# Attention in a transformer layer: two neighbouring score tiles of a first-half unit share one score buffer, one bank each

## The chip, the cores and the metric

The kernel runs on one core of a Trainium2 chip. The core's engines are named as in the profile: PE (TensorE, matmuls), DVE (VectorE), ACT (ScalarE), POOL (GpSimd) and SP (SyncE, which issues the DMAs here); PEld is PE's loading of weights. The metric is the device time of one execution in microseconds (us); the median over several runs is compared.

## The reference

One layer of an encoder for 1024 rows of 1024 values: adaptive normalisation, a mixer with two kinds of attention heads, a channel MLP. The change lies in the attention heads, which compute, cut to what matters:

```
# 8 latent heads (MLA), query/key width 96, value width 64; chunks of 64 rows, chunk-causal mask
s = q @ k.T * 96**-0.5;  s = where(key_chunk <= query_chunk, s, -1e30)
o = softmax(s) @ v
# 8 banded heads, width 64; each chunk sees itself and the 8 chunks before it, with a bias by distance
s = q @ k_band.T * 64**-0.5 + bias;  o = softmax(s) @ v_band
```

Everything is float32. Matmul operands are split into a high and a low part, and a product is made of three matmuls (high by high, high by low, low by high).

## The kernel before, in words

The sequence is cut into eight tiles of 128 query rows. A *unit* is one head and one half of the sequence: the first half (`u.g == 0`) has the tiles i = 0 to 3, the second half the tiles 4 to 7. There are 16 first-half and 16 second-half units. The banded units come first (`c00`, `c01`, ... in names: head pair, then odd or even head), then the latent units (`m00` to `m13`: group of four heads, then head). Halves and heads follow each other in the list `tiles`, and a loop calls `u.scores(i)` for tile n and, three tiles later, `u.values(i)` for a pair of tiles. Each call is followed by `pace`, which puts matmuls of other projections (the fillers: `ipq`, `ipv`, `mp`, `qu`, `ku`, `oc`) into the stream by the cost of what was just issued.

`Unit.scores` makes one tile: matmuls of queries by keys into a score buffer in PSUM (`s`), for query tile i over (i − lo + 1) × 128 keys; on DVE the mask and a minimum over the row (lines 810 to 822; the scores are kept negated); on ACT the exponential with a row sum (line 829); a reciprocal on DVE; a scaled float16 high part on POOL (line 73) and its low part on DVE (line 851); and a DMA that transposes both (line 863) into a tile `PT` that a pair of query tiles shares. `Unit.values` multiplies a pair's transposed tiles by the values on PE (line 891). After the last pair, ACT and DVE take the result out (lines 900 and 901) and a DMA stores it.

A score buffer is 1024 columns of float32, two PSUM banks of 512. There are two such buffers (tag `S`, `bufs=2`), which take four of the eight banks. A tile of a first-half unit has at most 512 columns and so fills at most the first bank of its buffer.

The order of instructions on each engine isn't the order of the code. A scheduler lays all instructions out with a timing model of its own, taking those of higher priority first: the calls of `tc.high_priority` lift scores by `OFF_S = 400` and the rest by 200. Each engine then works its list off strictly in order, and semaphores hold an instruction until what it needs is done. A buffer of a pool is handed to the next tile of its tag when the last reader of the tile before is done. Between two uses of one tile the framework adds the waits that it finds necessary.

The attention lies between 86 and 612 us of the span: banded heads up to about 340 us, latent heads from about 375 us.

## Time and profile before

| | |
|---|---|
| median of 3 runs | 1333.68 us (1331.05 to 1333.88) |
| profiled execution | 1334.5 us, span 1332.7 us |
| mean granted TensorE clock | 0.958 |
| instructions | 18710 |

The page's first part gives each engine's busy time and share of the span. In the rows by stage each engine has its busy time and count, and behind them the granted clock of PE (1.00 is full speed), the mean busy share of the DMA engines and the bandwidth. In a row of waits stand the waiting instruction, what released it, the total in us, how often, and the longest. In the timeline a row gives the start, how long it took, the engine and line, the output and inputs, a count of merged instructions, and in brackets the idle time before it and what ended it. A matmul's duration contains its way through the array; successive matmuls overlap.

### The profile page before, as it was taken

Reading aid. Unit: us, or ns where it says so; the run is one execution under the profiler, and the core shown is the slowest. Engines: PE = TensorE matmul, PEld = TensorE weight load, DVE = VectorE, ACT = ScalarE, POOL = GpSimd, SP = SyncE. Lnnn points to the kernel's source line nnn. Section 1 sums busy time; section 2 is a strip of 40 time slices with the busy share of each in tenths; the row PEclk is TensorE's granted clock in tenths of the full one; section 3 lists DMA queues with packets and bytes.
Section 4 is the critical chain, followed back from the end, with each engine's and each line's share of the span. In section 5 each row is a group of like instructions: output and inputs, shape, how many; then the busy total and the mean of one; then the engine's idle time right before and its main releaser. Section 6 shows DMA issues by size and latency. Waiting matters only on the chain.

```text
span 1332.7 us, 18710 instructions
## 1 busy us (share of the span) xinstructions
PE 1212.8 (91%) x6168; PEld 997.1 (75%) x6168; DVE 1088.7 (82%) x1928; ACT 622.3 (47%) x1132; POOL 572.3 (43%) x610
## 2 busy tenths in 40 slices
PE   3899999989667798888889999999999998999998
PEld 3888878868555576666677888888888886888886
DVE  6979898877589967894779888898889986687667
ACT  5454654445555545553366444444443444443331
POOL 5476773675675633354615445444444541000000
PEclk9899999989878798997999999999999998999999
DMA  8416768766123685879702333333333336943441
GB/s 321 144 55 156 164 143 197 150 151 138 35 72 70 119 172 122 152 164 326 275 16 79 106 124 111 122 116 108 113 106 132 111 119 221 393 151 114 132 159 63
DMA packets 223689, 190.57 MB, mean 143 GB/s; under 512 B 148708, under 2 KB 166884, under 8 KB 223592
## 3 DMA queue, kind: packets, MB, share of 16 engines
q1 hardware_dynamic: 223592, 189.38, 50.3%
q8 instruction: 48, 0.79, 0.3%
q14 instruction: 49, 0.40, 0.1%
HBM read 117.24 MB, written 37.49 MB: 116 GB/s over the span
## 4 chain that ended last, share of the span: by engine, by line
PE 48%; DVE 3%; DMA 2%; issue 1%; ACT 1%; POOL 0%; SPq 0%; POOLq 0%; DVEq 0%
PE p L1125 10%; PE p L1126 10%; PE p L1127 10%; PE dnA_P L1460 2%; PE dnA_P L1461 2%; PE dnA_P L1462 2%; PE dnB_P L1461 1%; PE dnB_P L1460 1%; PE dnB_P L1462 1%; PE dnA L1461 1%; PE dnA L1460 1%; PE dnA L1462 1%; PE dnB L1461 1%; PE dnB L1462 1%; PE dnB L1460 1%
## 5 line engine op out<-in xcount | busy, mean ns | idle before, releaser
L77 ACT ACTIVATE dnP<-dnr 128x1024 fp32r<-128x1024 f32 x73 | 77.4, 1064 | 117.5 <-PE dnA_P L1462 46.4
L1434 DVE TENSOR_TENSOR dnP<-dnr,dnP 128x1024 fp32r<-128x1024 f32 x72 | 87.9, 1224 | 52.7 <-ACT dnP L77 47.7
L73 POOL TENSOR_SCALAR hlm<-Pm,rim 128x512 f16<-128x512 f32 (+2 forms) x96 | 65.4, 691 | 77.5 <-DVE rim L832 32.0
L84 POOL TENSOR_TENSOR wf<-wu,wf 128x512 fp32r<-128x512 f32 x22 | 39.8, 1808 | 118.2 <-ACT wf L77 118.2
L1296 DVE SCALAR_TENSOR_TENSOR u<-c,cvp,u 128x1023 f32<-128x1023 f32 x44 | 58.6, 1372 | 27.8 <-ACT u L1295 27.8
L84 POOL TENSOR_TENSOR wb<-wu,wb 128x512 fp32r<-128x512 f32 x22 | 42.2, 1920 | 75.0 <-ACT wb L77 59.6
L73 POOL TENSOR_SCALAR hlc<-Pc,ric 128x640 f16<-128x640 f32 (+2 forms) x64 | 48.0, 753 | 54.5 <-DVE ric L832 25.8
L851 DVE SCALAR_TENSOR_TENSOR hlm<-Pm,rim,hlm 128x512 f16<-128x512 f32 (+2 forms) x96 | 65.9, 696 | 5.5 <-POOL hlm L73 5.2
L829 ACT ACTIVATE Pc<-sc,mc 128x640 f32<-128x640 f32 (+2 forms) x64 | 42.2, 660 | 55.2 <-DVE mc L818 26.1
L891 PE MATMUL pvm<-PTm,vt 128*128 128x256 f16 (+1 forms) x320 | 47.7, 302 | 22.1 <-DMA PTm<-hlm 14.2
L829 ACT ACTIVATE Pm<-sm,mm 128x128 f32<-128x128 f32 (+3 forms) x64 | 47.1, 738 | 37.7 <-DVE mm L822 21.2
L1295 ACT ACTIVATE u<-c,cvp 128x1024 f32<-128x1024 f32 x44 | 52.4, 1238 | 26.0 <-DVE c L1394 18.0
L1297 DVE SCALAR_TENSOR_TENSOR u<-c,cvp,u 128x1022 f32<-128x1022 f32 x44 | 61.7, 1442 | 0.0
L891 PEld LDWEIGHTS <-vt 128*128 128x128 f16 x320 | 33.1, 111 | 37.0 <-issue 21.6
L77 ACT ACTIVATE wc<-ws 128x512 fp32r<-128x512 f32 x21 | 13.3, 632 | 91.9 <-DVE ws L1144 86.1
L154 PE MATMUL ipq<-wq_s,hT 128*128 128x256 f32 x192 | 55.7, 290 | 0.0
L156 PE MATMUL ipq<-wq_s,hT 128*128 128x256 f32 x192 | 55.4, 288 | 0.0
L155 PE MATMUL ipq<-wq_s,hT 128*128 128x256 f32 x192 | 55.1, 287 | 0.0
L851 DVE SCALAR_TENSOR_TENSOR hlc<-Pc,ric,hlc 128x640 f16<-128x640 f32 (+2 forms) x64 | 49.2, 774 | 6.8 <-POOL hlc L73 6.7
L1461 PE MATMUL dnA_P<-dnP 128*128 128x512 f32 x132 | 51.3, 389 | 0.0
L1462 PE MATMUL dnA_P<-dnP 128*128 128x512 f32 x132 | 51.3, 389 | 0.0
L1460 PE MATMUL dnA_P<-dnP 128*128 128x512 f32 x132 | 51.2, 389 | 0.0
(442 smaller groups left out, 4413.7 us busy)
## 6 DMA issues: line engine op xcount, KB each, us to landing
wu<-w_up SPq DMA_DIRECT2D x44, 512.0 KB, 3.5
dnr<-g_d SPq DMA_DIRECT2D x73, 256.0 KB, 2.8
aw<-w_ada SPq DMA_DIRECT2D x48, 256.0 KB, 3.4
g_d<-u SPq DMA_DIRECT2D x22, 512.0 KB, 3.0
dnr<-w_down SPq DMA_DIRECT2D x44, 256.0 KB, 5.4
adaw<-w_ada_a SPq DMA_DIRECT2D x16, 512.0 KB, 6.0
x<-x SPq DMA_DIRECT2D x16, 512.0 KB, 9.8
g_d<-gs SPq DMA_DIRECT2D x22, 256.0 KB, 2.8
```

The costliest lines, as they stand in the source:

```text
L73: pool.tensor_scalar(o, i, s, 1.0, op0=MUL, op1=MUL)
L77: act.activation(o, i, AF.Copy)
L84: (pool if eng == "p" else dve).tensor_tensor(o, i, f32(hi), op=SUB)
L829: act.activation(pr[:, :n], sv, AF.Exp, bias=m[:], scale=-1.0, accum_out=rsum[:, 0:1])
L851: dve.scalar_tensor_tensor(hl[:, w:2 * w], pp, ri[:], hl[:, :w], op0=MUL, op1=SUB)
L1125: pe.matmul(pt, sh, pg[:, 0], start=(k == 0 and not add), stop=False, skip_group_check=skip)
L1126: pe.matmul(pt, sh, pg[:, 1], start=False, stop=False, skip_group_check=skip)
L1127: last = pe.matmul(pt, sl, pg[:, 0], start=False, stop=(k == 3), skip_group_check=skip)
L1434: r = f(*a, **k)
L1460: pe.matmul(pt, sh, w[:, 0, 0], start=start, stop=False, skip_group_check=add)
L1461: pe.matmul(pt, sh, w[:, 1, 0], start=False, stop=False, skip_group_check=add)
L1462: pe.matmul(pt, sl, w[:, 0, 0], start=False, stop=stop, skip_group_check=add)
```

## The change

In a first-half unit (i below 4) a buffer is taken only for the even tiles. The odd tile that follows writes the second half of the same buffer, which is its other bank. Second-half units keep one buffer for each tile. Nothing else is edited, and no matmul or transfer is added or left out.

```
-                s = ps.tile([P, 1024], F32, name=f"s{nm}", tag="S", bufs=2)
+                if i >= 4 or i % 2 == 0:
+                    u.s = ps.tile([P, 1024], F32, name=f"s{nm}", tag="S", bufs=2)
+                s = u.s if i >= 4 else u.s[:, i % 2 * 512:(i % 2 + 1) * 512]
```

The later lines move down by two (797 becomes 799, 803 becomes 805, 891 becomes 893). The scheduler lays everything from the first score tile to the end of the attention out anew. In the rows below, a name is followed by the unit and the query tile: `sc00_2` is the score buffer that was taken for tile 2 of unit `c00`. The size at the end tells the tile: 128 columns for tile 0, 256 for tile 1, 384 for tile 2, 512 for tile 3. What an instruction waits for stands in brackets where there is something: a counter of an engine (`Activation_49` is ACT's) or of a DMA queue.

The first unit of the banded heads on PE, before:

```order
L797 MATMUL sc00_0_904<-k0_0_897,qh0_0_0_888 128x128 [waits Activation_49,Pool_49]
L797 MATMUL sc00_0_904<-k0_0_897,ql0_0_890 128x128
L797 MATMUL sc00_1_926<-k0_0_897,qh0_0_0_888 128x256
L797 MATMUL sc00_1_926<-k0_0_897,ql0_0_890 128x256
L154 MATMUL ipv0_4_1026<-wv0_s0_518,hT0_0_1_259 128x256
...
L155 MATMUL ipv0_4_1026<-wv0_s0_518,hT0_0_1_259 128x256
L797 MATMUL sc00_2_949<-k0_0_897,qh0_0_0_888 128x384 [waits Activation_49]
L797 MATMUL sc00_2_949<-k0_0_897,ql0_0_890 128x384
```

And now:

```order
L799 MATMUL sc00_0_904<-k0_0_897,qh0_0_0_888 128x128 [waits Activation_49,Pool_49]
L799 MATMUL sc00_0_904<-k0_0_897,ql0_0_890 128x128
L799 MATMUL sc00_2_948<-k0_0_897,qh0_0_0_888 128x384
L799 MATMUL sc00_2_948<-k0_0_897,ql0_0_890 128x384
L154 MATMUL ipv0_4_1024<-wv0_s0_518,hT0_0_1_259 128x256
...
L154 MATMUL ipv0_4_1024<-wv0_s0_518,hT0_0_1_259 128x256
L799 MATMUL sc00_0_904<-k0_0_897,qh0_0_0_888 128x256 [waits Activation_49]
L799 MATMUL sc00_0_904<-k0_0_897,ql0_0_890 128x256
```

Tiles 1 and 2 have changed places: tile 2 follows tile 0 at once, and tile 1, which now lies in tile 0's buffer, waits on ACT's counter. The count that it waits for is that of tile 0's exponential.

The start of unit `m12` (a latent head, near 554 us) on PE, before:

```order
L803 MATMUL sm12_0_7029<-mk12_0_6946,mq12_0l_6938 128x128
L803 MATMUL sm12_1_7060<-mk12_0_6946,mq12_0h_6937 128x256 [waits Activation_49]
...
L803 MATMUL sm12_1_7060<-mk12_0_6946,mq12_0l_6938 128x256
L154 MATMUL oc6_0_7187<-wo4_0_5355,ch6_7183 128x512
...
L803 MATMUL sm12_2_7094<-mk12_0_6946,mq12_0h_6937 128x384 [waits Activation_49]
...
L803 MATMUL sm12_2_7094<-mk12_0_6946,mq12_0l_6938 128x384
L891 MATMUL pvm11_1_7045<-PTm11_4_0_6896,vt1_0_4955 128x256 [waits PE_49]
...
L891 MATMUL pvm11_1_7045<-PTm11_4_1_6901,vt1_4_5213 128x256 [waits DMAHW1_49]
```

And now:

```order
L805 MATMUL sm12_0_7001<-mk12_0_6918,mq12_0l_6910 128x128
L729 MATMUL mq13_0_ps_7193<-ident_68,qn1_0_4937 96x128 [waits DVE_49,PE_49]
...
L893 MATMUL pvm11_1_7017<-PTm11_4_0_6868,vt1_0_4939 128x256 [waits Activation_49]
...
L893 MATMUL pvm11_1_7017<-PTm11_4_1_6873,vt1_4_5195 128x256 [waits DMAHW0_49]
...
L805 MATMUL sm12_2_7065<-mk12_0_6918,mq12_0h_6909 128x384 [waits PE_49,Activation_49]
...
L805 MATMUL sm12_0_7001<-mk12_0_6918,mq12_0h_6909 128x256 [waits Activation_49]
...
L805 MATMUL sm12_0_7001<-mk12_0_6918,mq12_0l_6910 128x256
L154 MATMUL oc6_0_7157<-wo4_0_5337,ch6_7153 128x512
```

The 12 value matmuls of unit `m11` (`pvm11_1`), which stood behind tiles 1 and 2 and six `oc` matmuls, now stand ahead of them, four transposes (`mq13_0_ps`) after tile 0. On DVE, ACT, POOL and SP the score tiles keep the order 0, 1, 2, 3, 4.

## The prediction

> **What bounds the kernel now.** I read the page's busy times and chain first, then the busy times by stage, then the waits of the stage that has slack, then that stage's timeline.

> ```profile
> span 1332.7 us, 18710 instructions
> PE 1212.8 (91%) x6168; PEld 997.1 (75%) x6168; DVE 1088.7 (82%) x1928; ACT 622.3 (47%) x1132; POOL 572.3 (43%) x610
> PE 48%; DVE 3%; DMA 2%; issue 1%; ACT 1%; POOL 0%; SPq 0%; POOLq 0%; DVEq 0%
> ```

> TensorE (PE) is busy 91% of the span and carries nearly all that the chain of waits attributes, so only what makes PE idle, or run at a lower clock, moves the end. The profiled execution took 1334.5 us, 1.8 more than its span and 0.8 more than the median of 1333.7. Busy times by stage (PE, weight loads, DVE, ACT, POOL, then granted clock, DMA share, GB/s):

> ```profile
> 86.00:150.00 64.00, 62.12 (x461) 55.16 (x460) 55.13 (x178) 32.80 (x78) 38.66 (x47) 1.00 0.61 146
> 150.00:210.00 60.00, 55.91 (x398) 47.85 (x397) 55.33 (x147) 35.55 (x85) 42.07 (x49) 0.97 0.75 156
> 210.00:275.00 65.00, 62.82 (x461) 55.03 (x459) 55.41 (x147) 28.80 (x71) 34.27 (x41) 1.00 0.76 175
> 275.00:340.00 65.00, 59.02 (x325) 49.37 (x326) 46.35 (x127) 31.97 (x105) 42.59 (x92) 0.95 0.61 134
> 375.00:455.00 80.00, 55.74 (x253) 41.98 (x253) 72.32 (x214) 44.49 (x106) 49.80 (x53) 0.80 0.39 84
> 455.00:505.00 50.00, 47.80 (x258) 38.39 (x256) 37.32 (x97) 23.42 (x49) 23.96 (x30) 0.95 0.77 164
> 505.00:612.00 107.00, 85.88 (x485) 67.57 (x486) 85.11 (x214) 52.39 (x110) 42.75 (x60) 0.90 0.76 154
> 612.00:1333.00 721.00, 700.40 (x3044) 570.10 (x3043) 588.10 (x593) 311.56 (x415) 231.78 (x160) 0.99 0.42 144
> ```

> The first four rows are the banded heads: PE is full, because other projections' matmuls stand between the score tiles. In 375–455 (first latent heads) DVE is busy 72.32 of 80 us, so DVE sets the pace. In 505–612 (last four latent heads) no engine is full: PE idles 21.1 us and DVE 21.9. That stage is a ring of waits between engines, and the order on PE decides there. From 612 on nothing of the change is left. The waits of PE in 375–612, of PE in 86–340, and of DVE in 505–612 (total us, times, longest):

> ```profile
> PE sm L803 <- ACT Pm L829: 16.3, 15, 2.3
> PE pvm L891 <- DMA PTm<-hlm: 14.2, 9, 3.3
> ...
> PE pvc L891 <- DMA PTc<-hlc: 4.5, 5, 1.9
> PE sc L797 <- ACT Pc L829: 3.1, 3, 1.8
> ...
> DVE sm L821 <- PE sm L803: 10.7, 8, 2.5
> ```

> PE waits for two things: a score buffer that the exponential (L829) has to clear, 16.3 us, and a transposed tile that a DMA has to land before the value matmuls (L891), 14.2 us. The last row closes the ring: DVE in turn waits for score matmuls.

> **The change, part by part.** No operation is added or removed; two orders change.

> *Waits.* Before, each tile waits for the exponential of the tile two before it. Now tiles 0 and 1 share one buffer. In the built program tile 1's first matmul waits for tile 0's exponential although it writes the other bank; tile 3 waits for tile 2's in the same way; tile 2 is free as soon as the other buffer is. So still two tiles are in flight, and PE takes them as 0, 2, 1, 4, 3 where DVE, ACT, POOL and SP keep 0, 1, 2, 3, 4 (SP's transposes among them, so no queue is passed). A tile whose scores are ready on PE one place early gains nothing, since the other engines take it in the old place; tiles 1 and 3 come one place late.

> *Term a, the last four heads.* The start of head m12, in the trace of before on PE, with the two transposes on SP that matter for it:

> ```profile
> 553.79 0.42 PE L803 MATMUL sm<-mk,mq_0h 96*128 96x128 f32 x2
> 554.05 0.27 PE L803 MATMUL sm<-mk,mq_0l 96*128 96x128 f32 x1
> 556.35 0.50 PE L803 MATMUL sm<-mk,mq_0h 96*128 96x256 f32 x2 [2.04 <-ACT Pm L829]
> 556.69 0.28 PE L803 MATMUL sm<-mk,mq_0l 96*128 96x256 f32 x1
> 556.82 0.40 PE L154 MATMUL oc<-wo,ch 128*128 128x512 f32 x1
> ...
> 558.99 0.62 PE L803 MATMUL sm<-mk,mq_0h 96*128 96x384 f32 x2 [0.61 <-ACT Pm L829]
> 559.45 0.33 PE L803 MATMUL sm<-mk,mq_0l 96*128 96x384 f32 x1
> 559.63 1.38 PE L891 MATMUL pvm<-PTm,vt 128*128 128x256 f16 x12
> 560.84 0.60 PE L729 MATMUL mk_ps<-ident,kn 128*96 128x128 f32 x4
> 561.24 0.72 PE L803 MATMUL sm<-mk,mq_0h 96*128 96x512 f32 x2
> ...
> 555.75 1.24 SPq L863 DMA_TRANSPOSE PTm<-hlm  x1
> 557.09 2.58 SPq L863 DMA_TRANSPOSE PTm<-hlm  x2
> ...
> DMA to landing us min/median/max: 2.3/3.0/5.2
> ```

> Before, tile 1 (256 columns), six `oc` matmuls and tile 2 (384 columns) stand ahead of the 12 value matmuls of m11 at 559.63. They cover its transposes: the first was issued at 555.75 and lands at 558.1 to 558.8 by the last row; the second, issued at 557.09, lands at 559.4 to 560.1. In the changed order only four transposes (0.60) stand between tile 0 and these value matmuls. PE comes to them at 554.3 + 0.6 = 554.9 and stands until 558.8; it runs eight, waits for the second piece, and is through at about 560.4. Queued behind it on PE are tile 2 (0.8), four transposes (0.6), tile 1 (0.8) and six `oc` (six steps from 556.82 to about 558.2, 1.4), so that block ends at 564.0. Before, the same work without four transposes (0.6), which came later, ended at 561.2. The loss is 564.0 − 561.2 − 0.6 = 2.2 us, with the two waits of 2.04 and 0.61 already credited. For those tiles DVE waits next (the 10.7 row).

> Value groups move ahead of score tiles in this way at three places of the stage: m11's tiles 1 and 2, m12's tiles 1 and 2, and m12's tiles 3 and 4. 3 × 2.2 = 6.6 us. The lower end is 0, if the ring settles into another rhythm in which the transposes are there; the upper is the whole stand of 3.9 at each, 11.7. I take 6.6, whose rows are this place's own.

> *Term b, 375–455.* DVE sets the pace and keeps its order of tiles: 0, between −2 and +2 (a PE wait of 2.3, the longest in its row, either way).

> *Term c, the score-buffer waits of 16.3 us.* Tiles 2 and 4 shed theirs, tiles 1 and 3 take them up one exponential later: 0 beside what term a credits.

> *Term d, the banded heads.* Tiles 1 and 3 move behind 20 to 30 filler matmuls, and their transposes land later against the same value matmuls. All waits of this kind there are 4.5 + 3.1 = 7.6 us. I take +2, about a quarter more; from −3 (the 3.1 gone) to +6 (nearly doubled). The cover is the fillers; the place where they are thinnest is 275–340 (PE 59.02 of 65).

> *Term e, the clock.* In 505–612 the granted clock is 0.90 beside 21.1 us of PE idle: 10.7 us of clock lost, 0.5 per idle us. For 6.6 more idle I take half of that rate, +1.6; ends 0 and 3.3.

> [...]

> Sum: 1334.5 + 6.6 + 0 + 0 + 2 + 1.6 = 1344.7; against the median, 0.8 lower, **1344 us**. By the ends of a to e it reaches from 1329 to 1357.

> **Rivals.**

> *A, the clock tips over: about 1358.* If the stands of 3.9 come in full (11.7 instead of 6.6) and drop 505–612 to the clock of 375–455, its PE work grows by 85.88 × (0.90/0.80 − 1) = 10.7: 1334.5 + 11.7 + 2 + 10.7 = 1358.9, 1358 against the median. For: 375–455 shows that clock with waits of this kind. Against: 455–505 has its clock at 0.95 next to it. It decides where the stage's clock falls below 0.85.

> *B, faster: about 1326.* The buffer waits vanish and the transposes hold. Between tile 0 and tile 1 of m12 there now stand value matmuls, tile 2 and eight transposes, 1.38 + 0.8 + 1.2 = 3.4 us, where tile 2's wait for the same exponential ended 4.7 us after tile 0; it is mostly covered. If half of the 16.3 goes (8.2) and a, d and e stay at 0, 1334.5 − 8.2 = 1326.3, against the median 1325.5. Against it: PE reaches the value matmuls earlier, and 14.2 us of waits there say that they are not ready. It decides where that row stays at 14 or less.

> [...]

> *C, nothing: 1334.* The change doesn't loosen what it seems to (two tiles in flight before and after), and only the order of equals is swapped: terms a, d, e cancel against the shed waits.

> **How the numbers follow.** A measurement of this kernel tells 0.2% (2.7 us) from no change. Forecast 0.56, A 0.14, B 0.22, C 0.08. Faster is B, same is C, slower the forecast and A: 0.22, 0.08, 0.70. The range from 1327 to 1358 holds the forecast's own 1329 to 1357, C, half of B (which spreads from 1322 to 1331: 0.11 left out) and half of A (1354 to 1362: 0.07 left out), so 0.18 is outside.

> **What would show it.** Right: in the profile after, PE's waits for transposes in the latent heads rise from 14.2 towards 21, the waits for the exponential stay near 16, DVE's wait for scores passes 10.7, stage 505–612 becomes 7 to 9 us longer, the banded heads about 2, 375–455 and all from 612 on stay. Term a is wrong if the value waits stay; d if the banded stages move by over 6 us; e if the last stage's clock stays at 0.90. The forecast falls if 375–455 moves by over 4 us, since I hold DVE to set its pace, or if the whole is below 1331.

## Result: 0.4% slower, and the profile after

The changed kernel takes 1338.82 us (median of 20 runs, 1333.99 to 1346.63) where the kernel before takes 1333.67 in the same comparison. The ratio is 1.0039, 95% interval 1.0025 to 1.0053: slower by 5.2 us. A second comparison gave 1.0032 (1.0014 to 1.0050). The forecast was 1344, with 0.70 on slower; direction and range held, the size was 5 us too large. Line numbers of the changed kernel are two higher from the score buffer on.

The profiled execution of the changed kernel took 1335.7 us, 3.1 under the median, so its stages show where time went, not all of it. First its whole and the page's busy times, then busy times by stage in the windows of the prediction (PE, weight loads, DVE, ACT, POOL, granted clock, DMA share, GB/s):

```profile
span 1333.9 us, 18712 instructions
PE 1213.6 (91%) x6168; PEld 996.4 (75%) x6168; DVE 1094.3 (82%) x1928; ACT 622.5 (47%) x1132; POOL 582.0 (44%) x610
```

```profile
375.00:455.00 80.00, 57.99 (x268) 43.93 (x267) 75.33 (x224) 45.96 (x108) 52.69 (x54) 0.78 0.41 88
455.00:505.00 50.00, 47.92 (x258) 38.59 (x255) 42.15 (x96) 24.23 (x50) 24.85 (x30) 0.94 0.73 160
505.00:612.00 107.00, 82.57 (x457) 64.59 (x457) 82.92 (x206) 49.53 (x104) 42.83 (x58) 0.90 0.67 138
612.00:1333.00 721.00, 701.71 (x3060) 570.52 (x3060) 586.63 (x595) 313.28 (x418) 233.17 (x160) 0.99 0.43 146
```

Windows fixed in time mislead once work has moved: at 612 the changed kernel is still in its last head. So here are the stages cut at events (first banded scores, first latent transposes, first output projection `op`, first feed-forward product, first `dn`), first of before, then of after:

```profile
86.20:357.90 271.70, 251.63 (x1688) 216.78 (x1687) 221.43 (x626) 139.65 (x360) 166.37 (x241) 0.96 0.64 145
357.90:611.70 253.80, 200.41 (x1044) 155.22 (x1041) 209.68 (x572) 130.33 (x288) 124.95 (x149) 0.88 0.60 125
611.70:664.20 52.50, 48.80 (x210) 38.98 (x208) 35.01 (x29) 18.17 (x32) 30.97 (x28) 0.95 0.87 332
664.20:1114.50 450.30, 439.71 (x1914) 356.61 (x1913) 397.08 (x410) 212.64 (x307) 196.28 (x129) 0.99 0.31 105
```

```profile
84.90:358.70 273.80, 253.79 (x1689) 218.02 (x1687) 224.73 (x626) 138.97 (x360) 170.37 (x241) 0.95 0.63 143
358.70:619.00 260.30, 202.31 (x1042) 156.35 (x1040) 216.56 (x573) 132.05 (x289) 129.05 (x149) 0.87 0.57 122
619.00:670.70 51.70, 49.00 (x208) 38.62 (x208) 35.65 (x29) 17.05 (x31) 29.82 (x28) 0.95 0.88 334
670.70:1116.40 445.70, 437.85 (x1915) 355.36 (x1913) 392.00 (x410) 212.72 (x307) 198.60 (x129) 1.00 0.32 105
```

The latent heads (second row) grow by 6.5 us: 4.6 more idle (260.30 − 202.31 against 253.80 − 200.41), the rest a lower clock. The feed-forward stage (fourth row), which the change does not touch, shrinks by 4.6. That is the shape of the result: most of the forecast loss came, and nearly as much was given back where I had said that nothing of the change is left.

The waits of PE in 375–615, of PE in 86–340 and of DVE in 505–612:

```profile
PE pvm L893 <- DMA PTm<-hlm: 22.6, 13, 4.4
PE sm L805 <- ACT Pm L831: 13.9, 13, 2.5
```

```profile
PE pvc L893 <- DMA PTc<-hlc: 9.6, 6, 3.4
```

```profile
DVE sm L823 <- PE sm L805: 5.1, 7, 1.3
```

The first row answers to 14.2 before: waits for transposed tiles rose to 22.6, as forecast. The second answers to 16.3. The DVE row answers to 10.7 and fell, against the forecast.

### The profile page after: what moved, and what is told of

Same layout as the page of the kernel before. It is cut to its first block, busy times and chain, and to the rows that moved or that the text cites. A ratio compares the mean times of both kernels' runs of the same rounds, so it can differ in the third digit from the quotient of the medians.

```text
span 1333.9 us, 18712 instructions
## 1 busy us (share of the span) xinstructions
PE 1213.6 (91%) x6168; PEld 996.4 (75%) x6168; DVE 1094.3 (82%) x1928; ACT 622.5 (47%) x1132; POOL 582.0 (44%) x610
## 5 line engine op out<-in xcount | busy, mean ns | idle before, releaser
L73 POOL TENSOR_SCALAR hlm<-Pm,rim 128x512 f16<-128x512 f32 (+2 forms) x96 | 69.1, 731 | 87.9 <-DVE rim L834 28.6
L1298 DVE SCALAR_TENSOR_TENSOR u<-c,cvp,u 128x1023 f32<-128x1023 f32 x44 | 55.8, 1309 | 27.6 <-ACT u L1297 24.8
L853 DVE SCALAR_TENSOR_TENSOR hlm<-Pm,rim,hlm 128x512 f16<-128x512 f32 (+2 forms) x96 | 69.9, 742 | 7.2 <-POOL hlm L73 6.9
L893 PE MATMUL pvm<-PTm,vt 128*128 128x256 f16 (+1 forms) x320 | 45.8, 294 | 22.6 <-DMA PTm<-hlm 22.6
L1297 ACT ACTIVATE u<-c,cvp 128x1024 f32<-128x1024 f32 x44 | 52.3, 1238 | 23.4 <-DVE c L1396 16.5
L853 DVE SCALAR_TENSOR_TENSOR hlc<-Pc,ric,hlc 128x640 f16<-128x640 f32 (+2 forms) x64 | 54.3, 856 | 9.4 <-POOL hlc L73 9.1
L154 PE MATMUL ipq<-wq_s,hT 128*128 128x256 f32 x192 | 56.7, 295 | 0.0
L1299 DVE SCALAR_TENSOR_TENSOR u<-c,cvp,u 128x1022 f32<-128x1022 f32 x44 | 55.5, 1301 | 0.0
## 6 DMA issues: line engine op xcount, KB each, us to landing
dnr<-g_d SPq DMA_DIRECT2D x73, 256.0 KB, 2.8
aw<-w_ada SPq DMA_DIRECT2D x48, 256.0 KB, 3.5
dnr<-w_down SPq DMA_DIRECT2D x44, 256.0 KB, 5.4
g_d<-gs SPq DMA_DIRECT2D x22, 256.0 KB, 2.8
```

Source lines behind the costliest of these rows:

```text
L73: pool.tensor_scalar(o, i, s, 1.0, op0=MUL, op1=MUL)
L154: pe.matmul(pt, sh, mh, start=(start and i == 0), stop=False)
L853: dve.scalar_tensor_tensor(hl[:, w:2 * w], pp, ri[:], hl[:, :w], op0=MUL, op1=SUB)
L893: last = pe.matmul(dst, u.vst(j), mov, start=(x == 0), stop=(x == len(todo) - 1), skip_group_check=True)
L1298: dve.scalar_tensor_tensor(u[:, 1:], c[:, :S - 1], cvp[:, cv + 1:cv + 2], u[:, 1:], op0=MUL, op1=ADD)
```

## Experiments

Stage lengths come from the profiled execution of each run, cut at the same events; idle is length minus PE busy; lost clock is half of the half-clock stretches in the stage; transpose waits are PE's waits for transposed tiles in the latent heads to their end.

| run | median us, ratio (95%) | banded | latent: length, idle, lost clock | transpose waits | feed-forward |
|---|---|---|---|---|---|
| before | 1333.7 | 271.7 | 253.7, 53.4, 29.6 | 14.2 | 450.3 |
| before_again | 1331.9, one run | 271.9 | 252.0, 52.5, 31.6 | 14.5 | 448.8 |
| after | 1338.8, 1.0039 (1.0025–1.0053) | 273.8 | 260.4, 58.0, 34.8 | 22.6 | 445.6 |
| after_again | 1337.3, 1.0032 (1.0014–1.0050) | 276.8 | 259.9, 55.8, 36.3 | 20.6 | 444.5 |
| e1_latent_only | 1332.5, 0.9997 (0.9983–1.0011) | 274.1 | 256.5, 56.0, 32.7 | 17.9 | 444.5 |
| e2_banded_only | 1326.7, 0.9950 (0.9933–0.9967) | 277.0 | 250.6, 48.0, 35.1 | 12.4 | 446.0 |
| e3_in_order | 1344.3, 1.0081 (1.0059–1.0104) | 274.2 | 265.7, 63.1, 40.9 | 20.3 | 446.5 |
| e4_before_values_first | 1347.5, 1.0108 (1.0088–1.0127) | 273.0 | 271.5, 60.5, 47.0 | 23.4 | 444.4 |
| e5_after_values_later | 1336.0, 1.0014 (0.9995–1.0033) | 277.2 | 255.8, 51.9, 35.8 | 16.7 | 446.4 |
| e6_before_adds_first | 1330.8, 0.9985 (0.9968–1.0002) | 275.0 | 251.2, 53.0, 28.2 | 10.9 | 447.7 |
| e7_after_scalings_first | 1338.4, 1.0034 (1.0012–1.0056) | 275.2 | 255.5, 54.8, 32.7 | 17.4 | 446.5 |
| e8_values_later_adds_first | 1334.8, 1.0003 (0.9985–1.0022) | 277.3 | 256.0, 56.2, 32.0 | 14.6 | 447.3 |
| e9_before_split_first | 1331.4, 0.9986 (0.9970–1.0002) | 277.4 | 251.5, 51.8, 31.4 | 13.0 | 446.9 |
| e10_one_place | 1337.4, 1.0039 (1.0020–1.0059) | 274.9 | 260.6, 56.7, 38.6 | 22.2 | 446.8 |

Across the runs the latent heads' length goes with the transpose waits, from 250.6 us at 12.4 to 260.6 at 22.2; e3 and e4 lie above that line, with 41 and 47 us of clock lost. before_again, e6 and e9 have the PE order of before all through the attention, and after_again and e7 that of after. So the table also shows what one order varies by: transpose waits of 10.9 to 14.5 and latent heads of 251.2 to 253.7 us with the order of before, 17.4 to 22.6 and 255.5 to 260.4 with that of after.

The theory: PE comes to value matmuls before their transposed tiles have landed, because the shared buffer lets the scheduler put value groups ahead of score tiles. Rivals: the wait of tile 1 for tile 0's exponential by itself; PE's order of tiles, 0, 2, 1, against that of the other engines; the clock alone.

**Which heads (e1, e2).** The sharing in the latent heads alone, and in the banded heads alone:

```
-if i >= 4 or i % 2 == 0:
+if u.band or i >= 4 or i % 2 == 0:          # e1; s = u.s there too
+if not u.band or i >= 4 or i % 2 == 0:      # e2; s = u.s there too
```

> Shared score buffers in the latent heads alone; the banded heads are as before. Theory (the loss comes from value matmuls that PE reaches before their transposed tiles, in the last four latent heads): 1338 to 1341 us, +4 to +7; PE's waits for transposes in the latent heads above 20 us. Rival 1 (the banded heads lose it): within 0.2% of 1334. Rival 2 (the whole difference is the granted clock, which falls differently for any new order): anything from -5 to +5, with the waits no guide to it.

> Shared score buffers in the banded heads alone; the latent heads' score tiles keep a buffer each. Theory: within 0.2% of 1334 (term d said +2), PE's waits for transposes in the latent heads near 14 us. Rival 1 (the banded heads lose it): +4 to +6, 1338 to 1340. Rival 2 (granted clock): anything from -5 to +5.

Both missed, in the same direction. The latent sharing alone gave no loss, the banded sharing alone was 0.5% *faster* than before, the fastest kernel here, and together they lose 0.4%: the parts do not add up. Both also have the shorter feed-forward stage (444.5 and 446.0). With that set aside, e1's latent heads are still 3 to 5 us longer than the two of before, and e2's are shorter. Rival 2 (the clock) allowed anything from −5 to +5, so e1's time doesn't rule it out; its idle time in the latent heads, 56.0 where the order of before has 51.8 to 53.4, speaks against the clock as the whole. e2's latent gain lies in the first four latent heads, whose tiles it doesn't share: 127.8 us, where the order of before has 134.6 to 135.2 and e1 136.4. So the banded heads' sharing also changes what comes behind them. (e2's profiled execution, 1330.2 us, is the slowest of its six.)

**Value groups put ahead by hand, and put back (e4, e5).** e4 is the kernel before, with a buffer for each tile; in the latent heads tile 1 is issued behind the value group traced last, tile 3 behind the first eight matmuls of the next. e5 is the changed kernel, with the value groups of the second halves traced one tile later and issued behind the newest score tile.

```
+with tc.issue_after(vlast[-1]) if i in (1, 3) and not u.band and vlast else ...:   # e4, score matmuls
     ...
+late.append((u, i))       # e5, latent, u.g == 1; run at the next tile:
+with tc.issue_after(slast[-1]):
+    v.values(j)
```

> The kernel before, a buffer for each tile, with one thing of the change's PE order put in by hand: in the latent heads score tile 1 is issued behind the first group of value matmuls of the head before, and tile 3 behind the first part of the second. Theory (the order of value matmuls on PE is the loss, the shared buffer only brings it about): +3 to +7, 1337 to 1341, waits for transposes above 20 us. Rival (the loss is the wait of tile 1 for tile 0's exponential, which this kernel does not have): within 0.2% of 1334.

> The changed kernel with the second-half value groups of the latent heads issued one score tile later on PE, behind tiles 1 and 3 of the next head as in the kernel before. Shared buffers and their waits stay. Theory: the loss goes, 1331 to 1336, waits for transposes in the latent heads at 15 us or less. Rival (the wait of tile 1 for tile 0's exponential is the loss): 1337 to 1341, unchanged.

e4 loses 14 us with no shared buffer at all, twice what was expected; its latent heads are 18 us longer. Its waits for transposes, 23.4 us, are little more than the changed kernel's 22.6, so they are not the price by themselves. Its waits for score buffers fell at the same time, from 16.3 to 2.5, and idle time rose by 7. What e4 shows besides is a lower clock (same columns as above):

```profile
375.00:455.00 80.00, 59.91 (x252) 44.68 (x250) 73.83 (x216) 45.44 (x105) 55.46 (x55) 0.74 0.37 84
455.00:505.00 50.00, 46.32 (x239) 37.40 (x240) 36.19 (x92) 21.15 (x46) 18.15 (x25) 0.87 0.69 150
```

0.80 and 0.95 before have become 0.74 and 0.87: 47.0 us of clock lost in the latent heads where before lost about 30. In e5 the shared buffers and their waits stay (14.1 us for the exponential), and the waits for transposes are 16.7 (15 or less was expected). Its time lies some 3 us below the changed kernel's, with an interval that just holds 1 but overlaps both of the changed kernel's. Its profile helps little: idle time, 51.9, is below the 54.8 to 58.0 that the changed order shows, but e7, with the changed kernel's own order through the attention, shows 17.4 of transpose waits and 255.5 us of latent heads beside e5's 16.7 and 255.8. The order of value groups is thus enough to bring a loss (e4); that putting them back takes part of this one away is likely, but not shown.

**The wait or the order of tiles (e3).** Shared buffers, but every tile behind a shared pair issued in the old order:

```
+with tc.issue_after(odd_s[-1]) if (i < 4 and i % 2 == 0 or i == 4) and odd_s else ...:   # score matmuls
```

> The changed kernel, with the score tiles kept in their old order on PE (0, 1, 2, 3, 4) by issue order alone; the shared buffer and the wait of tile 1 for tile 0's exponential stay, and value groups still stand between tile 0 and tile 1. Theory (value matmuls ahead of their transposes): most of the loss stays, 1335 to 1342 us, waits for transposes in the latent heads at 17 us or more. Rival (the loss is PE taking tiles as 0, 2, 1, 4, 3 while the other engines keep 0 to 4): 1327 to 1332.

It is slower still, by 10.3 us. The rival that blames the order 0, 2, 1 by itself falls, since the old order with shared buffers is no faster. The theory's range was missed too (1342 at most). The shared wait doesn't show as the price: e3's waits for the exponential are 10.7 us, fewer than the changed kernel's 13.9. What grew is idle time (63.1) and lost clock (40.9), and as the edit lays out everything anew from the first banded unit on, why e3 is slower than the changed kernel stays open.

**The stage behind the attention (e6, e9, e7).** The scheduler's new layout reaches 60 us past the attention. On DVE before, the scalings of row tiles 5 and 6 come ahead of the residual add of tile 7 and of the split (`b<-hv,b`) that PE waits for; after, the add and the split come first. DVE in the first microseconds of the stage, which begins at 664.2 before and 670.7 after:

```profile
665.03 3.46 DVE L1193 TENSOR_SCALAR x<-x,r 128x1024 f32<-128x1024 f32 x2
668.42 2.28 DVE L1186 TENSOR_TENSOR x<-x,pa 128x1024 f32<-128x1024 f32 x1
670.62 1.28 DVE L84 TENSOR_TENSOR b<-hv,b 128x512 fp32r<-128x512 f32 x2
...
680.25 0.69 DVE L1222 TENSOR_TENSOR hv<-hv,hv 128x512 f32<-128x512 f32 x1 [5.45 <-ACT hv L1089]
```

```profile
671.35 2.29 DVE L1188 TENSOR_TENSOR x<-x,pa 128x1024 f32<-128x1024 f32 x1
673.56 1.78 DVE L84 TENSOR_TENSOR b<-hv,b 128x512 fp32r<-128x512 f32 x1
675.26 1.40 DVE L1195 TENSOR_SCALAR x<-x,r 128x1024 f32<-128x1024 f32 x2
...
681.82 0.69 DVE L1224 TENSOR_TENSOR hv<-hv,hv 128x512 f32<-128x512 f32 x1 [1.15 <-ACT hv L1091]
```

From the stage's start, the split begins at 6.4 before and 2.9 after, and `hv` comes at 16.0 before (14.5 in before_again) and 11.1 after. PE's waits for the split in this stage, before and after:

```profile
PE c_g L1126 <- DVE b L84: 4.2, 2, 2.5
```

```profile
PE c_g L1128 <- DVE b L84: 1.9, 2, 1.6
```

They fell by 2.3 us, and PE's idle time in the stage by 2.7, from 10.6 to 7.9. e6 puts the two scalings behind the add in the kernel before; e9 behind the split as well; both leave all that lies ahead as it was. e7 puts the scalings back ahead of the adds in the changed kernel.

```
+if t in (5, 6): continue                       # e6: scaled with tile 7,
+with tc.issue_after(add.ins): ...              #     behind its add
+with tc.issue_after(lo_ins["b11", 1].ins): ... # e9: tiles 5, 6 behind the split
+with tc.issue_after(scaled[...].ins): ...      # e7: adds of 4, 6, 7 behind scalings
```

> The kernel before with one thing put in by hand that the change brought along behind the attention: at the start of the feed-forward layer DVE issues the scalings of row tiles 5 and 6 behind the residual add of tile 7. Theory (the change also gives 4 to 6 us back there, which the prediction did not see): 1327 to 1330 us, the feed-forward stage 445 to 446 us where it was 450.3, its idle time near 8 us where it was 10.6. Rival (that stage's difference is where the granted clock happened to fall in the profiled runs): within 0.2% of 1333.

> The kernel before, attention untouched, with DVE's order at the start of the feed-forward layer as the changed kernel has it: residual add of tile 7 and the split of the operand that PE needs first go ahead of the scalings of tiles 5 and 6. Theory (the change gives time back there): 1327 to 1330.5 us, feed-forward stage 444 to 446.5, idle time there near 8. Rival (the stage's difference was the clock in one profile; the adds-first run gave only 3 us): 1331 to 1334.

> The changed kernel with the order of before put back on DVE at the start of the feed-forward layer: scalings ahead of the residual adds of tiles 4, 6 and 7 (one split of the first operand stays ahead of the last scaling). Theory (4 to 6 us were given back there): 1341 to 1345 us. Rival (clock): 1337 to 1340, unchanged.

In e6 and e9 the stage takes 447.7 and 446.9, short of the 4 to 6 us that were expected: the order accounts for 2 to 3 of the 4.6 us in the stage. The whole kernels gain 1.9 to 2.0 us by their ratios, each with an interval that just holds 1. Both medians lie above the theory's range and inside the rival's, so by the time alone the rival, the clock, would do as well; the idle times below tell the two apart. e7 missed: it stays at the changed kernel's time. There the split could not be put back (it starts 1.2 us into the stage), only the add is late, and the stage stays at 446.5. So it is the split that counts, not the add, and not `hv` either, which comes at 13.5 in e7 and at 12.5 and 11.7 in e6 and e9. PE's idle time in the stage follows its wait for the split through all five: 4.2 us of wait and 10.6 idle before, 3.2 and 9.6 in e6, 2.3 and 8.7 in e9, 2.1 and 8.5 in e7, 1.9 and 7.9 after. The rival has a part too: the rest of the 4.6 is lost clock, 4.6 us before and 1.8 after (2.9 and 1.1 in the second profiles); what makes that differ was not isolated.

**One place (e10).** In the changed kernel, one group of twelve value matmuls, of the fourth latent head, put behind tiles 2 and 1 of the fifth, in the way of e5:

```
+if i == 5 and u.nm == "m03" and u.g: late.append((u, i))
```

> The changed kernel with one value group moved: the twelve value matmuls of the fourth latent head's third pair are issued behind score tiles 2 and 1 of the fifth head, where the changed kernel has them ahead of both; the order behind it shifts a little. Theory (value groups ahead of score tiles are the loss, and this place carries most of it): the fifth head takes 22 to 25 us where it took 28.3, and the kernel 1333 to 1336.5. Rival (the shared buffer's wait slows the head whatever the order): 28 us and 1337 to 1341.

The fifth head did what was expected: 23.5 us. The kernel did not: 1.0039, as without the edit. In its profile the last head (m13) now takes 24.7 us where it took 18.7 to 18.9, so what one place gained the scheduler's new layout lost elsewhere. The next section shows that the edit also moved another group, the one that stood longest.

**Values later and adds first, from before (e8).** The kernel before with the value groups of e5 and the scalings of e6:

```
+if i % 2 and not u.band and u.g and u is not units[-1]: late.append((u, i))
+if t in (5, 6): continue                       # as in e6
```

> The kernel before with two edits: value groups of second-half latent tiles one score tile later, and the adds of the feed-forward start ahead of the scalings; a candidate that beats both. Theory: the second edit gives 4 to 6 us as it does alone; the first takes some of the 14.2 us of waits for transposes, 0 to 5: 1323 to 1330 us. Rival (values later only move the wait to the next score buffer): no better than the second edit alone.

No gain over e6: the waits for transposes stay at 14.6 us (14.2 before), those for score buffers are 18.0 (16.3 before), and the latent heads take 256.0. The rival was right.

**Both kernels again.**

> The changed kernel itself, once more, for a second profile and more times: 1337 to 1340 us; latent heads 255 to 261 us, feed-forward stage 445 to 446.5. If the loss were clock alone, the idle times of the latent heads would agree with before (53).

> The kernel before itself, for a second profile: feed-forward stage 449 to 451 us with 10 to 11 us idle if its order makes it so; 445 to 447 if the first profile's clock did.

Both feed-forward stages came out just below what was expected, 448.8 and 444.5, and as far apart as in the first profiles. The four profiles agree on what the order makes: feed-forward idle time 10.6 and 10.6 before, 7.9 and 7.8 after; latent idle time 53.4 and 52.5 before, 58.0 and 55.8 after. By means of the two profiles each, after minus before is banded +3.5, latent +7.3, projection and feed-forward −5.8, all else −0.9: together +4.1, beside 5.2 and 4.3 (0.32% of 1332.6) in the two comparisons.

## Why the prediction came out high

**Term a (6.6) and term e (1.6): right in kind, too small, and near the sum by luck.** Together 8.2, for the last four latent heads. Before's program through the attention has four profiles (before, before_again, e6, e9: latent heads 252.1 on average), after's three (after, after_again, e7: 258.6): +6.5. Idle time is +3.5 of it where a said 6.6; lost clock is +4.4 by the same records where e said 1.6, above its upper end of 3.3 (the two overlap by 1.4). e's own test, the clock of 505–612, read 0.90 as before: a window fixed in time did not see what moved across 612. That +6.5 lies near 8.2 is luck: the last four heads, for which a and e were meant, lost 11.5 us (92.7 to 104.2, from m10 to `op`), and the first four, for which I had 0, gave back 5.1 (134.9 to 129.8).

By head (from each head's first transpose on SP to the next head's; means of the four and the three profiles):

| | to first | 1 | 2 | 3 | 4 | 5 (m10) | 6 (m11) | 7 (m12) | 8 (m13) | end |
|---|---|---|---|---|---|---|---|---|---|---|
| before | 24.5 | 45.6 | 35.2 | 25.8 | 28.4 | 22.2 | 23.1 | 22.5 | 19.7 | 5.3 |
| after | 24.5 | 42.5 | 34.1 | 27.1 | 26.2 | 28.5 | 23.0 | 26.1 | 18.8 | 7.8 |

The prediction's three places were one in m11 and two in m12. m11 lost nothing, m12 3.6 by the means (the forecast was 4.4; 24.3 to 28.0 in the three profiles of after); the largest loss, 6.3, is in m10, where I counted none. In the trace of after on PE, at m10:

```profile
521.24 0.98 PE L805 MATMUL sm<-mk,mq_1h 96*128 96x512 f32 x4
522.06 0.57 PE L805 MATMUL sm<-mk,mq_1l 96*128 96x512 f32 x2
522.47 0.60 PE L729 MATMUL mk_ps<-ident,kn 128*96 128x128 f32 x4
526.27 1.68 PE L893 MATMUL pvm<-PTm,vt 128*128 128x256 f16 x8 [3.20 <-DMA PTm<-hlm]
527.70 2.06 PE L805 MATMUL sm<-mk,mq_1h 96*128 96x512 f32 x4
```

Tile 6's scores, four transposes, then m10's own second value group *ahead of tile 7*. It stands 3.20 us for tile 3's transposes; tile 3 is one of the tiles that the change makes late. Tile 7 then comes at 527.70, at half clock (2.06 for the four where they take 1.10 in e1 below). By the means of the four and the three profiles, m10 has 3.7 us more idle time (2.0 to 5.7) and 2.9 us more lost clock (0.9 to 3.8): together 6.6, beside the 6.3. In e1, in the trace of the same place, tile 7 goes first and nothing stands:

```profile
527.72 1.07 PE L805 MATMUL sm<-mk,mq_1h 96*128 96x512 f32 x4
528.63 0.57 PE L805 MATMUL sm<-mk,mq_1l 96*128 96x512 f32 x2
...
530.84 1.10 PE L805 MATMUL sm<-mk,mq_1h 96*128 96x512 f32 x4
531.77 0.61 PE L805 MATMUL sm<-mk,mq_1l 96*128 96x512 f32 x2
533.62 0.94 PE L893 MATMUL pvm<-PTm,vt 128*128 128x256 f16 x8
```

Its fifth head takes 23.8 us. That is the likeliest reason why e1's last four heads take only 95.6 us: the banded heads' new order shifts the latent heads' fillers, and with them this one group. e10 has the group behind tile 7 as well, so its 23.5 cannot tell the group it moved from this one. The other runs fit: where the group comes ahead of tile 7 and PE stands 2.1 to 3.3 us, m10 takes 28.3 to 28.7 (after, after_again, e7); where it comes ahead and PE stands 1.6 us or not at all, 23.4 to 25.0 (e5, e4, e8); where it comes behind, 21.6 to 23.9 (the order of before, e1, e2, e10). Only e3 is apart: 27.3 with the group behind, with 6.1 us of clock lost there. The step that failed is the count of places: I compared the two orders only where a value group crossed tiles 1 to 4 of the next head, and not inside m10.

At m12 the first stand that I priced at 3.9 was 0.35, the second 2.82:

```profile
556.66 1.36 PE L893 MATMUL pvm<-PTm,vt 128*128 128x256 f16 x12 [0.35 <-DMA PTm<-hlm]
565.46 1.05 PE L893 MATMUL pvm<-PTm,vt 128*128 128x256 f16 x8 [2.82 <-DMA PTm<-hlm]
```

The end costs 2.5 more, since `op` waits for an operand that is split late:

```profile
613.11 3.38 PE L893 MATMUL pvm<-PTm,vt 128*128 128x256 f16 x16 [4.40 <-DMA PTm<-hlm]
619.03 0.80 PE L154 MATMUL op<-wo,oh 128*128 128x512 f32 x1 [2.54 <-ACT oh L77]
```

**Term b (0 ± 2): wrong.** The first two latent heads, about 375 to 455, became 4.2 us *shorter* by the means (45.6 + 35.2 to 42.5 + 34.1), at the bound of 4 that I set as a point against the forecast: 80.2 to 81.2 in the four profiles, then 77.3, 77.3 and 75.0. The step that failed is "DVE sets the pace, so 0". DVE is the busiest engine there, but it was idle for 7.5 of these 80 us in before, and for 3.8 in after. What filled its idle time stays open. The sharing in these heads by itself isn't shown to do it: over the first four heads e1, which shares there, gained nothing (136.4), and e2, which shares in the banded heads alone, gained most (127.8; 134.9 before, 129.8 after). So the gain comes with the banded heads' new order. DVE's wait for scores in 505–612, which I had passing 10.7, fell to 5.1 (6.2 in after_again, 8.6 in before_again).

**Term c (0): nearly right.** Score-buffer waits went from 16.3 to 13.9 and 13.7.

**Term d (+2): its mechanism came, its size is not resolved.** Before's program shows 271.7, 271.9, 275.0 and 277.4 us for the banded heads, after's 273.8, 276.8 and 275.2: +1.3 between the means, inside a spread of 5.7 for one and the same program. e1, e4 and e8 have the banded heads of before too, and e2, e5 and e10 those of after; over all, it is 274.3 to 275.8, +1.5. PE's waits for transposes there rose, 5.8 to 9.4 by the same means (4.5 to 7.2 and 8.3 to 9.9). But PE's idle time as a whole did not (21.3 to 20.4), so others shrank; lost clock grew, 12.4 to 16.3.

**"From 612 on nothing of the change is left": wrong, and with the first four latent heads the largest miss.** It is worth −4.6 us in the feed-forward stage. It takes no shared buffer: e4, which has none, shows 444.4 there, as any new layout of the attention so far has shown 444 to 448 us. 10.3 − 4.6 is 5.7, beside 5.2 measured; that this closes is luck too, since +11.5 and −5.1 stand where I had +8.2 and 0. The order there had changed in the built program on PE and DVE; I read it only as far as the last head.

**Rivals.** A did not come (0.90 in 505–612, 0.85 was its point). In e4 the clock did fall with another order of value groups, but in 375–505 (0.74 and 0.87 where before has 0.80 and 0.95), and 505–612 stayed at 0.89. B did not: the built program holds tiles 1 and 3 for the exponential of the tile before, and the transpose waits rose where B needed them at 14 or less. A kernel without that wait was not run, so what more than two tiles in flight would give is not shown. C's cancelling did happen, between stages, and not in full.

## What to carry to other kernels

Where a scheduler lays out the program, an edit of one buffer is an edit of every order behind it: compare the two programs to the last instruction, and cost each place where an instruction that waits now stands ahead of one that was ready. A part's time alone says little then (0.0%, −0.5%, together +0.4%), so test a mechanism by forcing the order at its place, and look at the whole stage as well as at the place. Cut stages at events, and profile the same program more than once before a few microseconds of one stage are believed.

## What the runs showed of the hardware

Behind the stand in m10, of 3.20 us in after and 2.11 in after_again, PE ran at half clock. The two profiles there, the stretch with the stand and the one behind it (columns as above, the clock behind the POOL entry):

```profile
522.50:525.60 3.10, 0.57 (x5) 0.32 (x3) 2.83 (x7) 0.99 (x2) 0.00 (x0) 1.00 1.18 132
525.60:532.40 6.80, 6.13 (x19) 4.79 (x20) 2.45 (x5) 2.46 (x4) 1.18 (x2) 0.50 0.22 48
```

```profile
529.70:533.10 3.40, 1.31 (x11) 1.16 (x12) 1.24 (x3) 0.93 (x3) 1.15 (x2) 1.00 0.93 97
533.10:536.50 3.40, 3.40 (x10) 2.63 (x9) 2.21 (x5) 2.12 (x4) 0.00 (x0) 0.50 0.17 39
```

Successive matmuls overlapped: in the trace of after, the `oc` matmuls that start at 552.66, 552.90, 553.13 and 553.36 take 0.39 us each and come 0.23 to 0.24 apart.
